# Layer 0's mixers: two PSUM banks for a head's output, two instead of three for transposed probabilities

## The chip, the cores and the metric

The kernel runs on one core of a Trainium2 chip. The metric is the device time of one execution in microseconds (us); smaller is better. Engines are named as in the profile: PE is TensorE's matmul, PEld its weight load, DVE is VectorE, ACT ScalarE, POOL GpSimd, SP SyncE, which issues the loads and stores.

## The reference

An encoder trunk of two layers on x of 2048 tokens by 1024, all in float32. Only layer 0 is touched by the change:

```python
def even_layer(x, norm_g, w_in, w_out, a_qn, a_kn, a_sinks, b_qn, b_kn, b_rel, cos, sin):
    h = rms_norm(x, norm_g)
    aq, ak, av, ag, bq, bk, bv, bg = jnp.split(h @ w_in, cuts, axis=-1)
    ...  # QK-norm of both mixers, rotary for A
    ya = sliding_window_sink_attention(aq, ak, av, a_sinks) * jax.nn.silu(ag)  # own + 2 chunks of 64
    yb = chunked_relbias_attention(bq, bk, bv, b_rel) * jax.nn.silu(bg)        # own + 8 chunks of 64
    return x + jnp.concatenate([ya, yb], axis=-1) @ w_out
```

Mixer A has 8 query heads over 2 key/value heads, mixer B 8 heads; a head has 64 dimensions. Layer 1 is a differential attention over all earlier chunks, with its own projections.

## The kernel before

Each float32 operand of a large matmul is split into a high half (rounded) and a low half (the rest), and a product is made of two or three matmuls of these. Layer 0 first projects (lines up to L470), then `_mix0` runs both mixers and the output projection; then comes layer 1.

`_mix0` goes over 4 blocks of 512 tokens, and in each over 16 heads, alternating two of A and two of B. A head has a score part and a value part. The score part (`scores_a`, `scores_b`) makes scores in PSUM (tiles mSA, mSB, L567 and L568), takes the row maximum on DVE (L617, L698), the exponential on ACT (L622, L704) and scales on POOL (L628, L706), into mPA and mPB. The value part (`values_a`, `values_b`) goes over the key tiles of 128: PE transposes up to four 128x128 pieces of probabilities into one PSUM bank (tile mtrA or mtrB, L656 and L721); `split_pt` has ACT write the high half (mptH, L573) and DVE the low half (mptL, L574), each into one of three buffers in SBUF; then two value matmuls, with the high half (L663, L725) and with the low half (L665, L726), add into the head's output (mOA or mOB), 128x512, one PSUM bank. After a head's last key tile `join` adds the two 64-row halves of the output: ACT copies one (mlow, L581), DVE adds the other (myt, L582). POOL multiplies by the gate (L587), and `split_y` makes myH and myL (L593, L594).

The output projection of the block before (tile mom, 24 matmuls a tile, L214 to L216, evicted by DVE at L486) and some late gate tiles (mlg) run beside this, as `side`. `pace` writes the program: it takes score parts, lets the value parts trail by LAG0 units, and adds side units by SHARE0. The order on each engine is then set by a scheduler, which places an instruction by its own reckoning of when its operands and its buffers will be there; a PSUM tile gets a bank of its pool when the bank's last reader is past. So the number of banks in a pool also moves the order. Each engine runs its list in order.

PSUM has eight banks, and `BANKS0` deals them out in `_mix0`: NS to scores, NTR to transposed probabilities, NO to a head's output, NM to the side work. In the last block, every other output tile of the projection (j odd) takes its bank from the pool of head outputs.

Of the kernel before, what the change touches and what calls it, by code (L numbers as in the profile page):

```python
# [85 lines left out]
class Trunk:  # L86
    LATE = 8
    AHEAD = 2
    BANKS0, LAG0, SHARE0 = (3, 3, 1, 1), 9, 0.85
    FIN = 18  # L90
    COMB = 5
    BANKS1, LAG1 = (4, 2, 1, 1), (20, 36, 36, 36)
# [1106 lines left out]
```

## Time and profile before

| what | value |
|---|---|
| median of 3 runs (lowest to highest) | 2917.48 us (2905.52 to 2921.39) |
| the profiled execution, and its span | 2905.78 us, 2903.8 us |
| mean granted clock of PE | 0.973 |
| layer 0's projection | up to about 604 us |
| layer 0's mixers and output projection | 604 to about 1209 us |
| layer 1 | from about 1210 us |
| PE's 128-column transposes of probabilities | 560 (B) + 248 (A) |

All durations below are from the one profiled execution. A line of the profile names line, engine, operation and tiles as out<-in; a wait names who waited and for whom. A matmul's duration in the trace contains a modelled tail that overlaps the next matmul, so the time that a matmul costs PE (its slot) is read from start to start.

### The profile page before, as it was taken

The numbers are of one execution on the slowest core, as the hardware profiler recorded it, in microseconds if no ns is written. First come the engines' busy times: TensorE is split into PE (matmuls) and PEld (weight loads), VectorE is DVE, ScalarE is ACT, GpSimd is POOL, SyncE is SP. The second block draws the span as 40 slices with busy tenths as digits, with TensorE's granted clock in tenths as the row PEclk, the third lists the DMA queues.
The fourth block names the chain that finished last, engine by engine and source line by source line (L and its number), as shares of the span: only waits on it lengthen the run. The fifth ranks groups of instructions, "written<-read, shape, count | busy, mean of one in ns | idle before, by whom it ended". The sixth has DMA issues, their size and how long they took to land.

```text
span 2903.8 us, 45243 instructions
## 1 busy us (share of the span) xinstructions
PE 2718.9 (94%) x13704; PEld 2244.2 (77%) x13704; DVE 1950.6 (67%) x4685; ACT 1597.0 (55%) x4135; POOL 1612.4 (56%) x1968
## 2 busy tenths in 40 slices
PE   6999999998899999899999999999999999899889
PEld 5788888887787888777788887777777777677667
DVE  7762385257787885598729861666667888879842
ACT  4443543367666665343344321667667777678752
POOL 4541251334544354267745640777777777789851
PEclk9999999999999999999999999999999999999999
DMA  4673344648877763567894454786777677668873
GB/s 149 226 245 138 117 137 131 198 131 236 217 196 178 193 175 109 189 218 235 264 298 167 131 175 146 235 225 188 203 215 215 188 228 213 173 170 250 209 227 116
DMA packets 408866, 555.83 MB, mean 191 GB/s; under 512 B 47152, under 2 KB 187184, under 8 KB 408624
## 3 DMA queue, kind: packets, MB, share of 16 engines
q1 hardware_dynamic: 408624, 552.96, 64.7%
q8 instruction: 109, 1.79, 0.3%
q14 instruction: 133, 1.09, 0.1%
HBM read 388.18 MB, written 164.63 MB: 190 GB/s over the span
## 4 chain that ended last, share of the span: by engine, by line
PE 71%; DVE 11%; DMA 10%; ACT 4%; issue 2%; POOL 1%; SPq 1%; DVEq 0%; ACTq 0%; POOLq 0%
PE p1mm L216 5%; PE p1mm L214 5%; PE p1mm L215 5%; PE p0mm L214 3%; PE p0mm L215 3%; PE p0mm L216 3%; PE cS L883 3%; PE cS L884 3%; PE ctr L931 3%; PE cG L214 2%; PE cG L216 2%; PE cG L215 2%; PE cO L940 2%; PE com L214 2%; PE com L215 2%
## 5 line engine op out<-in xcount | busy, mean ns | idle before, releaser
L890 ACT ACTIVATE cP<-cS,cnm 128x512 f32<-128x512 f32 (+3 forms) x640 | 398.0, 628 | 147.3 <-DVE cnm L887 99.9
L887 DVE TENSOR_REDUCE cnm<-cS 128x1 f32<-128x512 f32 (+3 forms) x640 | 375.3, 600 | 98.1 <-PE cS L884 93.1
L304 POOL TENSOR_TENSOR p0wL<-p0ws,p0wH 128x512 fp32r<-128x512 f32 (+1 forms) x128 | 155.5, 1247 | 271.3 <-ACT p0wH L303 261.9
L883 PE MATMUL cS<-ck,cqd 128*128 128x512 f32 (+3 forms) x640 | 264.5, 417 | 42.4 <-ACT cP L890 19.0
L214 PE MATMUL p1mm<-p1wH,p1hH 128*128 128x512 f32 x768 | 303.1, 396 | 0.7 <-ACT p1wH L303 0.7
L215 PE MATMUL p1mm<-p1wL,p1hH 128*128 128x512 f32 x768 | 303.3, 395 | 0.4 <-POOL p1wL L304 0.4
L216 PE MATMUL p1mm<-p1wH,p1hL 128*128 128x512 f32 x768 | 303.6, 396 | 0.0
L918 POOL TENSOR_TENSOR cP<-cP,cP 128x512 f32<-128x512 f32 (+3 forms) x256 | 285.1, 1135 | 0.3
L304 POOL TENSOR_TENSOR p1wL<-p1ws,p1wH 128x512 fp32r<-128x512 f32 x128 | 167.6, 1329 | 140.5 <-ACT p1wH L303 116.1
L884 PE MATMUL cS<-ck,cql 128*128 128x512 f32 (+3 forms) x640 | 238.0, 376 | 7.0 <-DMA cql<-qL 6.9
L214 PE MATMUL p0mm<-p0wH,p0hH 128*128 128x512 f32 (+1 forms) x640 | 237.7, 374 | 3.5 <-ACT p0vt L454 2.6
L215 PE MATMUL p0mm<-p0wL,p0hH 128*128 128x512 f32 (+1 forms) x640 | 238.1, 373 | 0.0
L216 PE MATMUL p0mm<-p0wH,p0hL 128*128 128x512 f32 (+1 forms) x640 | 237.8, 373 | 0.1
L935 DVE TENSOR_TENSOR cptL<-ctr,cptH 128x512 fp32r<-128x512 f32 (+1 forms) x320 | 190.7, 599 | 51.3 <-ACT cptH L934 50.5
L934 ACT ACTIVATE cptH<-ctr 128x512 fp32r<-128x512 f32 (+1 forms) x320 | 169.9, 538 | 67.5 <-PE ctr L931 66.5
L912 POOL TENSOR_SCALAR cP<-cP,ccs 128x512 f32<-128x512 f32 (+3 forms) x288 | 191.9, 684 | 0.0
L883 PEld LDWEIGHTS cS<-ck,cqd 128*128 128x128 f32 x640 | 124.7, 195 | 83.1 <-ACT cP L890 42.3
L931 PE MATMUL ctr<-ident,cP 128*128 128x128 f32 x1088 | 175.9, 277 | 5.5 <-DVE cP L915 3.7
L917 POOL TENSOR_SCALAR cP<-cP,ccs 128x512 f32<-128x512 f32 (+3 forms) x256 | 170.6, 679 | 0.0
L214 PEld LDWEIGHTS p1mm<-p1wH,p1hH 128*128 128x128 f32 x768 | 145.8, 190 | 29.8 <-ACT p1wH L303 1.0
L215 PEld LDWEIGHTS p1mm<-p1wL,p1hH 128*128 128x128 f32 x768 | 145.6, 190 | 29.9 <-POOL p1wL L304 0.8
L216 PEld LDWEIGHTS p1mm<-p1wH,p1hL 128*128 128x128 f32 x768 | 145.8, 190 | 29.1 <-issue 0.2
(325 smaller groups left out, 7767.5 us busy)
## 6 DMA issues: line engine op xcount, KB each, us to landing
p1ws<-in_od_w_in_dram SPq DMA_DIRECT2D x56, 512.0 KB, 4.9
p0ws<-in_ev_w_in_dram SPq DMA_DIRECT2D x48, 512.0 KB, 4.3
ck<-kH SPq DMA_DIRECT2D x160, 128.0 KB, 4.4
ck<-kL SPq DMA_DIRECT2D x160, 128.0 KB, 4.4
cvH<-vH SPq DMA_DIRECT2D x80, 256.0 KB, 4.8
cvL<-vL SPq DMA_DIRECT2D x80, 256.0 KB, 4.3
cqd<-qH SPq DMA_DIRECT2D x128, 128.0 KB, 4.7
cql<-qL SPq DMA_DIRECT2D x128, 128.0 KB, 4.5
```

Of the source, the lines that this page charges most:

```text
L214: mm(ps, aH, bH, start=first, stop=False)
L215: mm(ps, aH, bL, start=False, stop=False)
L216: mm(ps, aL, bH, start=False, stop=last)
L304: nc.gpsimd.tensor_tensor(l[:, :width], ws[:, k, :width], f32(h[:, :width]), ALU.subtract)
L883: mm(ps, qd[:, m, js], kt[:, :wd], start=True, stop=False)
L884: self.anchor = mm(ps, ql[:, m, js], kt[:, :wd], start=False, stop=True).ins
L887: nc.vector.tensor_reduce(nm[:, m, z:z + 1], ps, AX.X, ALU.max, negate=True)
L890: nc.scalar.activation(chunks[z][:, :wd], ps, AF.Exp, bias=nm[:, m, z:z + 1], accum_out=acc)
L912: nc.gpsimd.tensor_scalar(p1, p1, c1, 1.0, ALU.mult, ALU.mult)
L918: nc.gpsimd.tensor_tensor(p1, p1, p2, ALU.add)
L931: nc.tensor.transpose(tp[:, (j - j0) * P:(j - j0 + 1) * P], us[j][kt // 4][:, kk:kk + P], self.ident)
L935: nc.vector.tensor_tensor(L[:, :wd], tp[:, :wd], f32(H[:, :wd]), ALU.subtract)
```

## The change

One tuple changes: the transposed probabilities get two banks instead of three, the heads' outputs two instead of one. Scores (3) and side work (1) keep theirs.

```diff
 class Trunk:
     LATE = 8
     AHEAD = 2
-    BANKS0, LAG0, SHARE0 = (3, 3, 1, 1), 9, 0.85
+    BANKS0, LAG0, SHARE0 = (3, 2, 2, 1), 9, 0.85
     FIN = 18
```

No instruction is added or removed; the scheduler gives another order from the first mixer heads to layer 1's start, and for a stretch near the end of layer 1.

First place: PE, where a head of A (mOA_8694) ends and a head of B (mOB_8793) begins, in the second block. Before (L721 transposes, L725 and L726 are value matmuls, L567 and L568 scores of another head):

```order
L665 MATMUL mOA_8694<-mptL_8765,mvA_7851 128x128
L721 MATMUL mtrB_8836<-ident_89,mPB_8542 128x128
L721 MATMUL mtrB_8836<-ident_89,mPB_8581 128x128
L721 MATMUL mtrB_8836<-ident_89,mPB_8633 128x128
L567 MATMUL mSB_9138<-mks_9085,mqd_9079 128x384
L568 MATMUL mSB_9138<-mks_9085,mql_9082 128x384
L721 MATMUL mtrB_8852<-ident_89,mPB_8542 128x128
L721 MATMUL mtrB_8852<-ident_89,mPB_8581 128x128
L721 MATMUL mtrB_8877<-ident_89,mPB_8542 128x128
L725 MATMUL mOB_8793<-mptH_8799,mvB_8536 128x512
L726 MATMUL mOB_8793<-mptL_8800,mvB_8536 128x512
```

Then L725 and L726 of the second tile follow, and those of mtrB_8836 (mptH_8840, mptL_8841). The same head in the new order:

```order
L725 MATMUL mOB_8793<-mptH_8799,mvB_8536 128x512
L726 MATMUL mOB_8793<-mptL_8800,mvB_8536 128x512
L721 MATMUL mtrB_8836<-ident_89,mPB_8542 128x128
L721 MATMUL mtrB_8836<-ident_89,mPB_8581 128x128
L721 MATMUL mtrB_8836<-ident_89,mPB_8633 128x128
L725 MATMUL mOB_8793<-mptH_8813,mvB_8536 128x512
L726 MATMUL mOB_8793<-mptL_8814,mvB_8536 128x512
L721 MATMUL mtrB_8852<-ident_89,mPB_8542 128x128
L721 MATMUL mtrB_8852<-ident_89,mPB_8581 128x128
L725 MATMUL mOB_8793<-mptH_8840,mvB_8536 128x384
L726 MATMUL mOB_8793<-mptL_8841,mvB_8536 128x384
```

The transposes of a tile have moved behind the first value matmuls of their head, and the value matmuls that use them stand two rows of other work later instead of a whole group.

Second place: ACT at the same head. Before:

```order
L573 ACTIVATE mptH_8799<-mtrB_8794 128x512
L573 ACTIVATE mptH_8813<-mtrB_8808 128x512
L581 ACTIVATE mlow_8787<-mOA_8694 64x512
L573 ACTIVATE mptH_8840<-mtrB_8836 128x384
L573 ACTIVATE mptH_8855<-mtrB_8852 128x256
```

And now:

```order
L573 ACTIVATE mptH_8799<-mtrB_8794 128x512
L581 ACTIVATE mlow_8787<-mOA_8694 64x512
L573 ACTIVATE mptH_8813<-mtrB_8808 128x512
L573 ACTIVATE mptH_8840<-mtrB_8836 128x384
L573 ACTIVATE mptH_8855<-mtrB_8852 128x256
```

The join of the head before stands one split earlier; it is still among the next head's splits.

Third place: DVE at the stage's end, where layer 1's rotary tables (p1tqC and so on) and layer 0's last evictions (L486) share the engine. Before:

```order
L187 TENSOR_TENSOR p1tkS_14942<-p1sin_14929,od_k_norm_103 128x16x32
L188 TENSOR_TENSOR p1tkS_14942<-p1sin_14929,od_k_norm_103 128x16x32
L486 TENSOR_TENSOR mxr_14651<-mom_14653,mxr_14651 128x512
L486 TENSOR_TENSOR mxr_14680<-mom_14682,mxr_14680 128x512
L191 TENSOR_SCALAR p1tqS_14933<-p1tqS_14933 128x16x32
```

And now:

```order
L187 TENSOR_TENSOR p1tkS_14942<-p1sin_14929,od_k_norm_103 128x16x32
L188 TENSOR_TENSOR p1tkS_14942<-p1sin_14929,od_k_norm_103 128x16x32
L191 TENSOR_SCALAR p1tqS_14933<-p1tqS_14933 128x16x32
L205 TENSOR_SCALAR p1xms_14957<-p1xss_14953 128x1
L193 TENSOR_SCALAR p1tqS_14933<-p1tqS_14933 128x16x32
L206 SCALAR_TENSOR_TENSOR p1xu_14958<-p1xy0_14956 128x1
L486 TENSOR_TENSOR mxr_14651<-mom_14653,mxr_14651 128x512
```

Four short rows of layer 1 have moved ahead of the first of these evictions.

## The prediction

> **What bounds the kernel now.** First the page: the span, the engines' busy time, and the shares of the chain that ended last.
>
> ```profile
> span 2903.8 us, 45243 instructions
> PE 2718.9 (94%) x13704; PEld 2244.2 (77%) x13704; DVE 1950.6 (67%) x4685; ACT 1597.0 (55%) x4135; POOL 1612.4 (56%) x1968
> PE 71%; DVE 11%; DMA 10%; ACT 4%; issue 2%; POOL 1%; SPq 1%; DVEq 0%; ACTq 0%; POOLq 0%
> ```
>
> PE sets the time. The change touches one stage only, so next comes the table of stretches: layer 0's mixers (604 to 1209 us), three slices of them, and a stretch near the kernel's end. Columns: stretch, length, busy time of PE, PEld, DVE, ACT and POOL, granted clock, DMA share, GB/s.
>
> ```profile
> 604.00:1209.00 605.00, 553.54 (x3280) 478.86 (x3279) 440.63 (x1502) 377.71 (x1003) 260.96 (x390) 0.96 0.70 182
> 750.00:780.00 30.00, 24.55 (x138) 21.54 (x139) 20.00 (x75) 14.62 (x35) 11.16 (x18) 0.89 0.74 205
> 780.00:810.00 30.00, 28.58 (x184) 25.07 (x183) 24.36 (x85) 20.95 (x57) 10.69 (x17) 1.00 0.73 192
> 1170.00:1209.00 39.00, 37.86 (x163) 31.17 (x164) 13.01 (x29) 4.92 (x12) 0.00 (x0) 0.91 0.35 125
> 2750.00:2800.00 50.00, 40.68 (x185) 31.24 (x186) 28.48 (x87) 32.38 (x89) 41.10 (x63) 0.90 0.73 202
> ```
>
> In the mixers PE is busy 553.5 of 605 us; DVE (441) and ACT (378) are behind it by far. So only what makes PE wait counts there. Who makes it wait, in the list of waits between 604 and 1160 us (total us, times, longest):
>
> ```profile
> PE mSA L567 <- ACT mPA L622: 7.6, 7, 2.1
> PE mOB L725 <- DVE myt L582: 6.6, 18, 0.9
> PE mom L216 <- POOL myL L594: 5.6, 1, 5.6
> PE mtrB L721 <- DVE mptL L574: 5.0, 13, 0.8
> PE mOB L726 <- DVE mptL L574: 0.9, 1, 0.9
> PEld mOB L725 <- DVE myt L582: 11.5, 21, 1.3
> PEld mtrB L721 <- DVE mptL L574: 9.0, 17, 1.1
> ACT mptH L573 <- PE mOB L725: 27.3, 25, 7.3
> ```
>
> The second row is the bank of a head's output: the first value matmul of a head (L725) waits until DVE has read the head before out of the single bank. The fourth is the bank of transposed probabilities: a transpose (L721) waits until DVE has made the low half (mptL) from the tile that stood there. The last shows that with three such banks ACT runs ahead of PE: 25 times its high half (mptH) waits for a buffer that an older value matmul still reads. The value matmuls therefore find their operands ready: the fifth row, 0.9 us, is the only one of them that waits for a half.
>
> **What the change removes.** Here is one of the 18 waits, in the timeline (start, us, engine, what, idle before):
>
> ```profile
> 789.30 0.22 PE L665 MATMUL mOA<-mptL,mvA 128*128 128x128 f32 x1
> 789.36 0.50 PE L721 MATMUL mtrB<-ident,mPB 128*128 128x128 f32 x3
> 789.57 0.59 ACT L581 ACTIVATE mlow<-mOA 64x512 f32<-64x512 f32 x1
> 789.61 0.42 PE L567 MATMUL mSB<-mks,mqd 128*128 128x384 f32 x1
> 789.87 0.33 PE L568 MATMUL mSB<-mks,mql 128*128 128x384 f32 x1
> 790.04 0.73 PE L721 MATMUL mtrB<-ident,mPB 128*128 128x128 f32 x3
> 790.19 0.49 ACT L573 ACTIVATE mptH<-mtrB 128x384 fp32r<-128x384 f32 x1
> 790.42 0.69 DVE L582 TENSOR_TENSOR myt<-mOA,mlow 64x512 f32<-64x512 f32 x1
> 791.14 0.56 DVE L574 TENSOR_TENSOR mptL<-mtrB,mptH 128x384 fp32r<-128x384 f32 x1
> 791.16 0.50 PE L725 MATMUL mOB<-mptH,mvB 128*128 128x512 f32 x1 [0.40 <-DVE myt L582]
> 791.73 0.39 PE L725 MATMUL mOB<-mptH,mvB 128*128 128x512 f32 x1
> 791.96 0.39 PE L726 MATMUL mOB<-mptL,mvB 128*128 128x512 f32 x1
> ```
>
> Mixer A's head ends at 789.30, is joined by ACT (0.59) and DVE (0.69), and only at 791.16 may the next head start. The same rows give PE's slots, start to start: 512 columns 0.23 us (791.73 to 791.96), 384 columns 0.17 (789.87 to 790.04), so 256 and 128 columns 0.12 and 0.06 in proportion. A transpose takes 0.11: three last 0.50, of which the last one's own length is 0.27:
>
> ```profile
> L721 PE MATMUL mtrB<-ident,mPB x560: 270/273/478, 619.1 to 1155.7; 128*128 128x128 f32 x187
> ```
>
> Slots between the two heads: six transposes and two of 384 columns, 6 x 0.11 + 2 x 0.17 = 1.0 us. The join needs 0.17 (a last matmul's length beyond its slot, 0.22 to 0.27 less 0.06 to 0.11) + 0.59 + 0.69 + 0.1 for hand-overs = 1.56. Shortfall 0.56, of which the trace counts 0.40 as idle, since 0.17 is still the last matmul's modelled length. So I add 0.17 to each counted wait: 6.6 + 18 x 0.17 = 9.6 us for the output bank (the weight loads' row says 11.5). With two banks the next head writes the other one; by the order a bank then comes round after 2.9 us of slots or more, so this goes to zero, all but the wait at the stage's end for the very last head.
>
> **What it adds.** The counts stay: 312 transposed tiles, 808 transposes, 752 value matmuls, no operation more or less. But a tile's bank must be empty two tiles later instead of three, and the order follows: transposes are issued later, next to the value matmuls that use them (the two orders of PE above show this on the very place of the rows just quoted). What was cover is gone. The chain of a tile, from these rows (idle in the last column):
>
> ```profile
> L573 ACT ACTIVATE mptH<-mtrB 128x512 fp32r<-128x512 f32 x56 | 32.7, 599 | 17.7 <-PE mtrB L721 11.4 <-PE mOA L663 6.1
> L573 ACT ACTIVATE mptH<-mtrB 128x384 fp32r<-128x384 f32 x56 | 27.4, 489 | 13.3 <-PE mtrB L721 5.2 <-DVE mptL L574 5.0 <-DVE mbnm L700 1.9
> L573 ACT ACTIVATE mptH<-mtrB 128x256 fp32r<-128x256 f32 x56 | 21.4, 381 | 26.3 <-PE mOB L725 24.2 <-PE mtrB L721 1.7
> L573 ACT ACTIVATE mptH<-mtrB 128x128 fp32r<-128x128 f32 x56 | 15.2, 271 | 8.2 <-PE mtrB L721 4.2 <-PE mOB L725 2.9
> L574 DVE TENSOR_TENSOR mptL<-mtrB,mptH 128x512 fp32r<-128x512 f32 x56 | 38.0, 689 | 14.3 <-ACT mptH L573 9.0 <-PE mOA L663 4.2
> L574 DVE TENSOR_TENSOR mptL<-mtrB,mptH 128x384 fp32r<-128x384 f32 x56 | 30.8, 551 | 3.4 <-ACT mptH L573 2.8
> L574 DVE TENSOR_TENSOR mptL<-mtrB,mptH 128x256 fp32r<-128x256 f32 x56 | 23.5, 419 | 9.2 <-ACT mptH L573 9.1
> L574 DVE TENSOR_TENSOR mptL<-mtrB,mptH 128x128 fp32r<-128x128 f32 x56 | 15.8, 283 | 5.2 <-ACT mptH L573 4.4 <-PE mOB L726 0.8
> ```
>
> High half: 0.17 + ACT + 0.07 = 0.83, 0.72, 0.62, 0.51 us for 512, 384, 256, 128 columns after the last transpose's slot. Low half: 0.17 + ACT + DVE + 0.1 = 1.55, 1.30, 1.07, 0.82. At the place shown, after the change the third tile (384 columns) has between its transposes and its high half's matmul two value matmuls of 512 and two transposes: 0.46 + 0.22 = 0.68 us against 0.72; the low half comes 0.17 later, at 0.85 against 1.30. So PE waits 0.04, then 0.41, where before it had 2 x 0.17 + 3 x 0.11 + 4 x 0.23 = 1.6 us of slots in between and waited for neither half.
>
> I did this count along all of the stage's some 3,280 PE rows in both orders: each row gets its slot, a row that comes too early for its tile's half, or for a bank, waits the shortfall, and all behind it moves. Before: 3 tile-bank waits of 2.9 us, 15 output-bank waits of 8.0, and 0.5 for halves: 11.4 us. After: 49 waits for a high half (7.5 us), 68 for a low half (20.0), and the one at the end (1.6): 29.1 us. Net +17.7, with each chain as short as its rows.
>
> They aren't that short. In the rows above the tile transposed at 789.36 gets its high half only at 790.19, since ACT first does the join's mlow, and its low half at 791.14, behind DVE's myt: from the end of its slots (789.69) to 791.70 are 2.0 us, against 1.30. That costs nothing before; in the new order the join still stands among the splits. Before's measured waits say how much longer a chain is on average: 9.6 (outputs) + 5.0 + 13 x 0.17 = 7.2 (tile banks) + 1.6 at the end = 18.4 us, which the count gives if every chain is 1.22 times its rows. With the same factor the new order counts 46.4 us. Net **+28 us**. Both ends: the chains as short as 0.82 of the rows (next part) give +11; the weight loads' 11.5 + 9.0 + 1.6 = 22.1 ask for a factor of 1.32, and the new order then has 56: +34; doubling for ACT and DVE being busier around the splits than a mean factor tells, at 1.5: 74.7 - 30.8 = +44.
>
> **Other moves.** At the stage's end layer 0's last output tiles now go over three banks instead of two. PE stops there in either order, because DVE has layer 1's rotary tables (L185 to L193) ahead of the evictions (L486):
>
> ```profile
> 1171.03 0.80 PE L214 MATMUL mom<-mw,myH 128*128 128x512 f32 x1 [5.87 <-DVE mxr L486]
> 1171.62 0.63 PE L215 MATMUL mom<-mw,myH 128*128 128x512 f32 x1
> ```
>
> After the last head PE has 30 rows before it needs an evicted bank, where it had 27: 3 x 0.23 = 0.7 us less idle; DVE has four short rows more in front of the first eviction. I cost the two at nothing together; the ends are the whole 5.87 gained and as much lost. SP's and POOL's issues are the same in number and change places; PE's waits for loads and for POOL aren't moved by a rule that I can see, so nothing, with the 5.6 us of the single wait for myL as the end on both sides. The last 100 us of layer 1 are ordered a little differently too; the idle 9.3 us of the 50 at 2750 bound what can be won or lost there.
>
> **The sum.** The profiled execution took 2905.8 us (2903.8 of it the span); with 28 us more, 2934. It lies at the lower edge of the runs, 11.7 under their median of 2917.5. Against the median the forecast is 2945.5, and I give that.
>
> **The rivals.**
> First, no change: the cover is longer than slots tell. The stage took 605 us for some 495 us of slots, so rows stand 605/495 = 1.22 times further apart than counted, which is the same as chains of 0.82 of their rows. The new order then waits 17.2 us, the old one 6.3 by the count but 18.4 as measured: between -1 and +11, about 2922. For it speaks that ACT is idle 37% of the stage; against it that stretch by idle time sits in a few gaps (5.87 and 5.6 in two places), not between a tile's transposes and its matmuls.
> Second, faster: the output bank's waits vanish and the splits hold up nobody, because ACT, no longer stopped by PE's late buffers (its 27.3 us), starts every split at once. The place is the three or four tiles at each head's change. It decides where chains fall below about 0.75 of their rows: the count gives 9.7 us at 0.7. At best 9.6 + 7.2 us go, 2917.5 - 17 = 2900. Against it: the join still shares ACT and DVE with the first tiles of the next head.
> Third, much slower: many short stops take PE's clock down. After the 5.87 us of idle just shown a matmul has 0.63 where the rows at 791 have 0.39, and its slice has a clock of 0.91; the slice at 750, just behind the 5.6 us wait, has 0.89. In the slice at 780, with the 0.40 wait in it, the clock is 1.00, so short stops did no harm there. If ten such slices of the stage fell to 0.89, they would lose 30 x 0.11 = 3.3 us apiece: 2945 + 33 = 2978.
> The Trainium skill (TensorE: Matmul & The Clock Gate, "A second HAM failure mode: psum-queue depth-cycling") states that cycling through PSUM banks can make PE pause between groups often enough for its clock to swing between half and full. By that rule the third rival is the likely one; the slice at 780 doesn't bear it out for pauses of this length.
>
> **How the numbers follow.** Chances: the forecast 0.54, no change 0.23, faster 0.11, much slower 0.12. A measurement of this kernel tells 0.5% (15 us) from no change; so slower 0.66, same 0.23, faster 0.11. The forecast's own range is +17.7 to +44, 2935 to 2962. The range takes in no change and the upper bound, and leaves out the better part of the faster rival (about 0.07, below 2910) and the worst of the much slower one (0.10, above 2972).
>
> **What would show it.** After: no PE row waits for myt but the one at the stage's end; new rows of PE (L725, L726, L663, L665) waiting for mptH and mptL, over 100 in number and 25 to 55 us in all with weight loads; ACT's 27.3 us for PE's buffers mostly gone; the stage some 630 us long, with PE's busy time about the same. I am wrong if these waits stay under 15 us, if the stage's clock falls clearly under 0.96, or if a difference of over 10 us comes from layer 1.

## The result, and the profile after

The changed kernel takes 2948.12 us (median of 6 runs, 2934.14 to 2951.8) against 2908.24 us for the kernel before in the same rounds (2901.79 to 2921.39). The ratio is 1.0112, with a 95% interval of [1.0083, 1.0142]: slower by 1.1%. Profiled a second time, with rounds of its own, it gave 1.0103 [1.0075, 1.0131] (below). The profiled execution took 2951.8 us.

The page's three lines after the change:

```profile
span 2950.0 us, 45103 instructions
PE 2746.1 (93%) x13704; PEld 2251.3 (76%) x13704; DVE 1941.1 (66%) x4685; ACT 1601.6 (54%) x4135; POOL 1614.8 (55%) x1968
PE 64%; DVE 12%; DMA 9%; ACT 5%; issue 2%; POOL 2%; SPq 1%; ACTq 0%; DVEq 0%; POOLq 0%
```

The span grew by 46.2 us. In the chain that ended last, PE's share fell from 71 to 64%, and ACT's, DVE's and POOL's rose by a point each. The stretches of the mixers, and the slice at 780 us (columns as before: stretch, length, busy PE, PEld, DVE, ACT, POOL, clock, DMA share, GB/s):

```profile
604.00:1238.00 634.00, 574.50 (x3284) 483.49 (x3283) 436.99 (x1507) 385.95 (x1008) 262.37 (x390) 0.97 0.68 176
780.00:810.00 30.00, 27.46 (x167) 22.92 (x167) 23.01 (x77) 19.31 (x52) 11.71 (x18) 1.00 0.80 197
```

From the first mixer matmul to layer 1's first one the stage takes 633.6 us, where it took 605.7: +27.9. (All stage lengths below are between these two rows of one profiled execution each.) The clock did not fall: 0.97 against 0.96. The slice at 780 got 167 PE rows done where it got 184.

Who makes PE and its weight loads wait there now (total us, times, longest):

```profile
PE mOA L665 <- DVE mptL L574: 11.4, 21, 1.4
PE mOB L726 <- DVE mptL L574: 5.6, 22, 0.6
PE mOB L725 <- ACT mptH L573: 5.2, 11, 2.1
PE mOA L663 <- ACT mptH L573: 3.0, 5, 0.7
PE mom L214 <- DVE mxr L486: 5.3, 1, 5.3
PE mom L214 <- DVE myt L582: 1.4, 1, 1.4
PEld mOB L726 <- DVE mptL L574: 19.6, 46, 1.2
PEld mOA L665 <- DVE mptL L574: 15.9, 22, 1.7
PEld mOB L725 <- ACT mptH L573: 12.7, 27, 2.4
PEld mOA L663 <- ACT mptH L573: 6.7, 16, 1.0
ACT mptH L573 <- PE mtrB L721: 73.5, 92, 5.0
```

The waits for the output bank are gone but one of 1.4 us, which is the stage's end. In their place stand waits of the value matmuls for their halves: 25.2 us in 59 waits on PE (before, one of 0.9), 54.9 us in 111 on the weight loads (before, 1.7). And ACT has changed sides: the 27.3 us of its idle time that ended when PE gave a buffer back are gone, and the row that ends when PE has made a tile grew from 22.4 to 73.5 us. ACT no longer runs ahead of PE.

A warning on reading this: PE's idle time in the stage hardly moved, 605.0 - 553.5 = 51.5 us before and 634.0 - 574.5 = 59.5 after, although the stage lost 28 us with the same work. The rest went into "busy", which rose by 21 us. The same head as in the prediction's timeline shows how:

```profile
793.61 0.39 PE L725 MATMUL mOB<-mptH,mvB 128*128 128x512 f32 x1
793.62 0.69 DVE L582 TENSOR_TENSOR myt<-mOA,mlow 64x512 f32<-64x512 f32 x1
793.84 0.40 PE L726 MATMUL mOB<-mptL,mvB 128*128 128x512 f32 x1
794.07 0.49 PE L721 MATMUL mtrB<-ident,mPB 128*128 128x128 f32 x3
794.32 0.48 PE L725 MATMUL mOB<-mptH,mvB 128*128 128x512 f32 x1
794.35 1.33 DVE L574 TENSOR_TENSOR mptL<-mtrB,mptH 128x512 fp32r<-128x512 f32 x2
794.60 0.49 ACT L573 ACTIVATE mptH<-mtrB 128x384 fp32r<-128x384 f32 x1 [0.49 <-PE mtrB L721]
795.09 0.51 PE L726 MATMUL mOB<-mptL,mvB 128*128 128x512 f32 x1 [0.29 <-DVE mptL L574]
795.44 0.38 PE L721 MATMUL mtrB<-ident,mPB 128*128 128x128 f32 x2
```

From the high half's matmul at 794.32 to the low half's at 795.09 are 0.77 us, where its slot is 0.23: 0.54 us lost. The trace shows 0.29 of it as idle; the rest is the 0.48 that the waiting pair's first matmul is drawn long. So short waits are read from start to start, or from the weight loads. The 54.9 us alone are not the loss, since other waits became shorter: all waits of the weight loads in the stage add up to 75.0 us before and 99.0 after, and this growth of 24.0 stands against the stage's 27.9. What is late here is DVE: it made myt, the join of the head before, from 793.62 to 794.31, and only then the two low halves.

A small part of the stage's loss is something else. Layer 1's first matmul (p1mm) waits for the high half of its weights (p1wH), which ACT makes; before, then after:

```profile
1210.64 0.96 PE L214 MATMUL p1mm<-p1wH,p1hH 128*128 128x512 f32 x3 [0.74 <-ACT p1wH L303]
1238.31 1.65 PE L214 MATMUL p1mm<-p1wH,p1hH 128*128 128x512 f32 x3 [3.34 <-ACT p1wH L303]
```

ACT now has two rows of layer 1's norm (L317) ahead of that half. From the last matmul of the output projection to this one the step is 6.4 us, where it was 4.2: 2.2 of the 27.9 us. So the new order doesn't end at layer 1's start: up to about 85 us into layer 1 the engines' rows are in another order too.

### The profile page after: what moved, and what is told of

The parts are those of the page before. It is cut to its first block, busy times and chain, and to the rows that moved or that the text cites. A ratio compares the mean times of both kernels' runs of the same rounds, so it can differ in the third digit from the quotient of the medians.

```text
span 2950.0 us, 45103 instructions
## 1 busy us (share of the span) xinstructions
PE 2746.1 (93%) x13704; PEld 2251.3 (76%) x13704; DVE 1941.1 (66%) x4685; ACT 1601.6 (54%) x4135; POOL 1614.8 (55%) x1968
## 4 chain that ended last, share of the span: by engine, by line
PE 64%; DVE 12%; DMA 9%; ACT 5%; issue 2%; POOL 2%; SPq 1%; ACTq 0%; DVEq 0%; POOLq 0%
PE p1mm L216 4%; PE p1mm L214 4%; PE p1mm L215 4%; PE cS L883 3%; PE cS L884 3%; PE ctr L931 3%; PE p0mm L214 3%; PE p0mm L215 3%; PE p0mm L216 3%; PE mom L214 2%; PE cG L214 2%; PE cO L940 2%; PE mom L216 2%; PE cG L216 2%; PE mom L215 2%
```

## Experiments

Each kernel changes the kernel before, except where it says otherwise. Ratios are against the kernel before in the same rounds, with their 95% intervals. The numbers in BANKS0 are the banks for scores, transposed probabilities, head outputs and side work.

**The changed kernel again**, for what an execution adds by itself.

> The changed kernel once more. In its first profile the mixers' stage (604 us to the first matmul of layer 1's projection) was 28 us longer than before, and layer 1 took 18 us more as well, though its instructions stand in the same order up to its last 100 us. If the stage's loss comes from the order of PE's rows, it is +26 to +30 again. If layer 1's 18 us belong to the kernel, they come again within 4 us; if they belong to that one execution, layer 1 differs by 8 us or more from the first profile.

Measured: 1.0103 [1.0075, 1.0131], 2939.32 against 2910.19 us. The stage took 631.7 us (+26.0). Layer 1's projection took 590.3 us (before 584.6, first profile of the change 589.1) and its attention 1111.5 (1108.6 and 1122.6). So of the 18.5 us that layer 1 had over before in the first profile 8.7 are left; the stage's loss stands.

**The transposes' bank alone taken away**, the output keeping its one bank:

```diff
-    BANKS0, LAG0, SHARE0 = (3, 3, 1, 1), 9, 0.85
+    BANKS0, LAG0, SHARE0 = (3, 2, 1, 1), 9, 0.85
```

> One part alone: two banks for transposed probabilities, still one for a head's output (an eighth bank lies idle). My theory (a tile bank less takes the cover between transposes and value matmuls): waits counted along the new order are 44 us with chains as short as their rows, of which 25 for the output bank, 10 for the halves and 8 for tile banks, and 66 us at 1.22 times; before they were 13 and 21. So the stage is 31 to 45 us longer than before, worse than with both parts. Rival (the second output bank is what hurts, since it lets heads' value parts run into each other): within 5 us of before.

Measured: 1.0154 [1.0117, 1.019], 2953.93 us, and a stage of 646.9 us, +41. Its stretch, then its waits:

```profile
603.00:1250.00 647.00, 574.81 (x3281) 482.42 (x3281) 439.19 (x1507) 382.41 (x1010) 261.21 (x390) 0.97 0.66 172
```

```profile
PE mOA L663 <- DVE myt L582: 23.3, 23, 2.2
PE mOB L725 <- DVE myt L582: 8.1, 12, 1.5
PE mOB L725 <- ACT mptH L573: 5.5, 26, 0.6
```

One bank less for transposes costs all of the loss and more. Most of it shows here as waits for the single output bank: 31.4 us, where they were 6.6. The value matmuls wait only 5.9 us for halves. Given two banks for transposes, the second output bank is worth 646.9 - 633.6 = 13.3 us. So the change can be read as a loss of 41 and a gain of 13, though the waits stand in other rows in the two kernels.

**The output's second bank taken from the scores** instead:

```diff
-    BANKS0, LAG0, SHARE0 = (3, 3, 1, 1), 9, 0.85
+    BANKS0, LAG0, SHARE0 = (2, 3, 2, 1), 9, 0.85
```

> The other part alone, its bank taken from the scores: banks (2, 3, 2, 1). My theory: waits for the output bank are gone, waits for halves are 3 to 8 us, and what it costs are score banks (8 to 15 us): 11 to 23 us in all against 13 to 21 before, so the stage is within 5 us of before. Rival (the second output bank hurts): value matmuls wait for mptH and mptL some 25 us as in the changed kernel, the stage 20 us or more longer.

Measured: 0.9946 [0.9924, 0.9968], 2893.0 us: faster, with a stage of 585.0 us (-20.7). That is better than expected. (The value matmuls' waits for halves, expected at 3 to 8 us, came to 14.5 on PE.) The stretch and the waits of this kernel:

```profile
604.00:1190.00 586.00, 548.10 (x3284) 474.94 (x3283) 437.39 (x1507) 377.04 (x1010) 261.43 (x391) 0.97 0.71 191
```

```profile
PE mOB L726 <- DVE mptL L574: 9.7, 14, 4.3
PE mSB L567 <- ACT mPA L622: 2.5, 5, 0.9
PE mSA L567 <- ACT mPA L622: 1.8, 3, 1.2
```

The expectation charged 8 to 15 us to the lost score bank. But the waits for score banks became fewer: 4.3 us in these two rows, where before the first of them was

```profile
PE mSB L567 <- ACT mPA L622: 6.1, 4, 2.6
```

and the second 7.6, in all 13.7. The two longest single waits of before are not in the new list either: 5.6 us for myL, and 5.87 at the stage's end. Why two score banks wait less than three was not tried; the other order is the likely place. What this run does show is that a second output bank doesn't hurt where the transposes keep three: PE has no wait for an output bank left. How much of the 20.7 us is that bank, and how much the other order, it doesn't show.

**The low half left out**, with the old banks (first) and the new ones (second). Transposed probabilities then have no low half, and both value matmuls read the high one:

```diff
-            L = sb.tile([P, 512], F32R, tag="ptL", name=n + "ptL", bufs=3)
...
-            nc.vector.tensor_tensor(L[:, :wd], ps[:, :wd], f32(H[:, :wd]), ALU.subtract)
-            return H, L
+            return H, H
```

> Banks as before (3, 3, 1, 1), and the low half of the transposed probabilities is left out: DVE's L574 is gone, and the second value matmul takes the high half again, so PE's rows keep their number and sizes. A tile's chain is ACT's copy alone, 0.83 us instead of 1.55 for 512 columns. It is the partner of the next run; counted waits 5 to 8 us. All theories expect the stage to be some 5 to 15 us shorter than before.

> The same with the changed kernel's banks (3, 2, 2, 1). My theory (the loss is the tile's chain ACT then DVE seen by PE): with the chain halved the counted waits are 7 to 13 us, 3 to 5 more than in the partner, so the stage is within 6 us of the partner's instead of 26 to 28 longer. Rival (the loss comes from the order itself or from the second output bank, whatever the chain): 20 us or more longer than the partner.

Measured, once each: 2873.1 us with the old banks, 2882.94 with the new; stages of 575.2 and 580.6 us.

```profile
604.00:1180.00 576.00, 539.49 (x3285) 475.12 (x3284) 322.47 (x1193) 378.35 (x1007) 260.52 (x391) 0.97 0.72 192
```

```profile
607.00:1188.00 581.00, 548.82 (x3283) 474.52 (x3282) 325.88 (x1194) 378.03 (x1007) 261.27 (x390) 0.98 0.72 190
```

```profile
PE mOB L723 <- ACT mptH L572: 5.0, 12, 1.5
PE mOA L661 <- ACT mptH L572: 3.2, 6, 0.9
```

With the chain cut to its first half the change costs 5.4 us, not 27.9. So most of the loss needs the whole chain of ACT and then DVE: neither the banks' cycling as such nor the transposes' being next to the value matmuls makes it alone. The 5.4 us are a net figure. The weight loads still wait 24.7 us in 58 waits for the high half (1.5 in the run with the old banks, 54.9 in the changed kernel), and against this the run with the old banks has waits that the other lacks, such as 7.1 us of PE for myL. DVE also has 118 us less to do in the stage here, which these two runs don't separate from the shorter chain.

**The join's reader of the bank on DVE freed from ACT.** ACT's copy of the lower rows and DVE's read of the upper ones were to run side by side, with the sum on POOL:

```diff
-            nc.vector.tensor_tensor(yt[hi, :], O[hi, :], tmp[hi, :], ALU.add)
+            nc.vector.tensor_scalar(yt[hi, :], O[hi, :], 1.0, None, ALU.mult)
+            nc.gpsimd.tensor_tensor(yt[hi, :], yt[hi, :], tmp[hi, :], ALU.add)
```

> Banks as before (3, 3, 1, 1), but the join frees the output bank sooner: ACT copies one half and DVE the other side by side, and POOL adds them from SBUF (64 instructions of POOL more, some 80 us of its time, of which it has 340 free in the stage). A bank comes free after 0.17 + 0.69 + 0.1 = 0.96 us instead of 1.56. If the 18 waits of PE for myt were worth their 9.6 us, they go nearly to zero (1 to 3 us left) and the stage gets 8 to 10 us shorter, 0.3%. Rival (such waits are only moved to the next wait, or POOL's longer chain to the gate holds up the output projection): the stage is within 2 us of before.

Measured: 1.0011 [0.9996, 1.0027], 2914.82 us, stage 604.9. Nothing was won, because the edit did not shorten the join. Its timeline at the same head (from L582 on, this kernel's lines are one higher than before's), and its waits:

```profile
833.81 0.60 ACT L581 ACTIVATE mlow<-mOB 64x512 f32<-64x512 f32 x1
834.44 0.68 DVE L582 TENSOR_SCALAR myt<-mOB 64x512 f32<-64x512 f32 x1
835.18 0.50 PE L726 MATMUL mOB<-mptH,mvB 128*128 128x512 f32 x1
```

```profile
PE mOB L726 <- DVE myt L582: 6.6, 18, 0.5
```

DVE reads other rows of the bank than ACT and needs nothing of ACT's, and still it starts 0.03 us after ACT ends (833.81 + 0.60). The 18 waits and their 6.6 us are what they were. The trace says who imposes the turn: DVE's read waits for a semaphore, a signal between engines, that ACT raises when it ends. None of the 64 reads begins before ACT's copy has ended, and in 11 of the waits DVE stood idle until then, 9.0 us in all. So the program orders the two reads; whether they could run side by side was not tried. The run says nothing on what a shorter join would bring.

**The join with a single reader of the bank.** ACT copies the whole output out of PSUM once; the rest is done from SBUF:

```diff
-            nc.scalar.activation(tmp[hi, :], O[lo, :], AF.Copy)
-            nc.vector.tensor_tensor(yt[hi, :], O[hi, :], tmp[hi, :], ALU.add)
+            nc.scalar.activation(tmp, O, AF.Copy)
+            nc.scalar.activation(yt[hi, :], tmp[lo, :], AF.Copy)
+            nc.gpsimd.tensor_tensor(yt[hi, :], yt[hi, :], tmp[hi, :], ALU.add)
```

> Banks as before (3, 3, 1, 1). The join in which DVE and ACT were to read the output bank side by side still had DVE start only when ACT had ended, and PE's 18 waits for myt stayed at 6.6 us, so it told nothing of their worth. Here ACT alone reads the bank, once, 128x512 (0.6 us), copies a half from SBUF again, and POOL adds. The bank is free after 0.17 + 0.60 + 0.07 = 0.84 us; DVE loses 64 instructions of 0.69 us, ACT gains 64 of 0.6. If the waits were worth their 9.6 us, PE has none of them longer than 0.2 us and the stage is 8 to 14 us shorter (counted waits 3 to 8 instead of 13 to 21). Rival (the time turns up in other waits, ACT's longer queue above all): within 3 us of before.

Measured: 0.9946 [0.9925, 0.9968], 2888.24 against 2906.79 us; stage 586.8 (-18.9).

```profile
604.00:1191.00 587.00, 543.56 (x3292) 476.54 (x3290) 411.53 (x1450) 410.47 (x1078) 341.42 (x454) 0.97 0.71 190
```

```profile
PE mOB L726 <- ACT mlow L581: 2.8, 5, 1.0
```

The output bank's waits fell from 6.6 to 2.8 us without a second bank, at 33 us more of ACT and 80 more of POOL, both off the path. The stage gained twice the 9.6 us that the prediction gave these waits. But not all of it is the bank. Of the two longest single waits of before, 5.6 us for myL and 5.87 at the stage's end, 0.4 and 2.2 us are left in their rows, while others came, one of 5.4 for a low half among them. DVE is also freed of the joins among the low halves. These were not taken apart.

**The same join with the changed banks**, (3, 2, 2, 1):

> The changed kernel's banks (3, 2, 2, 1) with the join in which ACT reads the output bank once and POOL adds. The join's DVE instruction no longer stands among the splits. My theory (the third tile bank was the cover): counted waits are 31 to 51 us against 3 to 8 in its partner with (3, 3, 1, 1), so its stage is 25 to 35 us longer than the partner's 586.8 us: 612 to 622. Rival (the changed kernel lost because the join of one head delays the next head's splits on DVE and ACT): with that taken away it is within 10 us of the partner.

Measured: 1.0056 [1.0037, 1.0074], 2920.68 against 2903.88 us; stage 615.7, that is +28.9 over the same join with the old banks.

```profile
PE mOA L666 <- DVE mptL L574: 15.7, 23, 2.0
PE mOA L664 <- ACT mptH L573: 7.4, 8, 1.5
PE mOB L727 <- DVE mptL L574: 4.7, 17, 1.4
PEld mOB L727 <- DVE mptL L574: 26.0, 69, 1.9
```

The join is no longer in DVE's way, and the waits for halves are more in sum: 28.7 us on PE where they were 25.2, 60.7 on the weight loads where they were 54.9. So the chain is late by its own length in an order that leaves it no cover; DVE's join among the splits is a part of single waits, as at 793.62 above, but not of the sum. ACT has a copy more for each head here, so this clears DVE's part of the join and not ACT's.

**A fourth transposes' bank**, from the scores:

```diff
-    BANKS0, LAG0, SHARE0 = (3, 3, 1, 1), 9, 0.85
+    BANKS0, LAG0, SHARE0 = (2, 4, 1, 1), 9, 0.85
```

> Banks (2, 4, 1, 1). Scores with two banks, transposed probabilities with four, one for outputs. The version (2, 3, 2, 1) had a stage 21 us shorter than before. If its gain came from the second output bank, this one lacks it: waits for myt are there again and the stage is within 5 us of before. Rival (its gain came from scores having two banks, which makes the scheduler space the heads otherwise, whatever the freed bank does): the stage is 15 us or more shorter here too.

Measured: 0.9982 [0.9963, 1.0], 2899.95 us; stage 594.9 (-10.8).

```profile
PEld mOB L725 <- DVE myt L582: 2.4, 4, 0.9
PE mtrB L721 <- POOL mPB L706: 11.6, 7, 3.8
```

This lies between what the two theories gave and does not tell them apart. The weight loads' waits for the output bank fell from 11.5 to 2.4 us in this row though it is still a single bank, and transposes issued earlier now wait for POOL's probabilities.

**The two gains together**: the join with a single reader and banks (2, 3, 2, 1).

> Both improvements together: banks (2, 3, 2, 1) and the join of ACT and POOL. With the short join the second output bank has little left to give (counted output waits 0 either way), and the score banks cost what they cost: stage between 575 and 590 us, thus about the better of the two alone (585.0 and 586.8). If the two gains were of different kinds and added up, it would be 566 us.

Measured: 0.9915 [0.9887, 0.9943], 2878.82 against 2903.88 us; stage 576.1. It is the fastest of the runs that keep the low half.

```profile
605.00:1182.00 577.00, 542.97 (x3284) 473.26 (x3283) 400.52 (x1443) 407.32 (x1074) 341.86 (x455) 0.98 0.71 194
```

| banks | join of before | join with a single reader |
|---|---|---|
| (3, 3, 1, 1) | 605.7 | 586.8 |
| (3, 2, 2, 1) | 633.6, 631.7 | 615.7 |
| (3, 2, 1, 1) | 646.9 | not run |
| (2, 3, 2, 1) | 585.0 | 576.1 |
| (2, 4, 1, 1) | 594.9 | not run |

Stage lengths in us. The step from the first row to the second is +28 and +29: there the join makes no difference. The step from the first to the fourth is -20.7 and -10.7: those two gains overlap.

## Why the prediction was right, and where not

- **The stage's term, +28 us: right.** It measured +27.9 and +26.0. The count with chains of their own rows gave +17.7 and was too low; the factor of 1.22 drawn from before's waits hit. There is luck in how well it hit. Measured as before's 18.4 us were, by PE's idle time and 0.17 for each wait, the new waits are 25.2 + 59 x 0.17 + 1.6 = 36.8, which makes +18. By the weight loads they are 54.9 + 1.5 = 56.4 against 22.1, which makes +34; that is what the count gave at a factor of 1.32. The stage lies between, and moves that the prediction put at nothing are in it: the scores' waits for ACT's mPA fell from 13.7 to 6.8 us on PE, the one for myL from 5.6 to 2.6, and the one for p1wH rose from 0.7 to 3.3.
- **The total: near, in part by luck.** 2945.5 was forecast and 2948.12 measured. But the forecast stood on before's first median, 2917.48; with the later rounds it is 2908.24. Of the 40 us between the medians (33 by the ratio) 28 were forecast; the rest lies in layer 1.
- **The mechanism: shown.** The new waits stand where they were forecast, at the value matmuls. Cutting the chain takes most of the loss away (+5.4); taking the join off DVE does not (+28.9). Taking the bank away alone costs more (+41), though there most of the waits are for the output bank.
- **Output bank, -9.6 us: the right kind, its size not shown.** The waits vanished as said. Beside two transposes' banks a second output bank was worth 13.3 us. With three, no run gave it by itself: (2, 3, 2, 1) also moves a score bank, and the 18.9 us of the single-reader join also have the two long waits in them that went.
- **"PE's busy time about the same": wrong.** It rose by 21 us, with the same matmuls at about the same clock (0.97 and 0.96), because part of each short wait is drawn as a long matmul, as at 794.32 above. The step that failed is the reading of the modelled tail: it was allowed for in the size of a wait (0.17 each; 111 x 0.17 would be 19 us), not in the busy time.
- **The place.** The wait was forecast on the third tile, 0.04 and then 0.41 us; it stands on the second tile's low half, 0.54 start to start, because DVE was still joining. The third tile's two matmuls follow at 795.58 and 795.83 without a wait. The count took DVE and ACT as free and put their being busy into one factor; that is good for a sum over a stage, not for a single place.
- **The stage's end, nothing: right for the evictions, not for the last step.** The stop was 5.87 us before and is 5.3 after. The 2.2 us in front of layer 1's first matmul were not forecast.
- **Layer 1, nothing: not borne out in full.** It took 18.5 us more in the first profile and 8.7 in the second. The rows of layer 1 from its start (columns as above), before and then after, split where its projection ends:

```profile
1210.60:1795.20 584.60, 574.13 (x2663) 473.04 (x2664) 402.43 (x700) 218.93 (x493) 332.93 (x256) 0.99 0.63 207
1795.20:2903.80 1108.60, 1019.47 (x4930) 812.28 (x4928) 786.76 (x1793) 738.87 (x2049) 806.61 (x1120) 0.96 0.72 204
```

```profile
1238.30:1827.40 589.10, 574.42 (x2663) 472.74 (x2664) 402.45 (x697) 217.16 (x490) 332.86 (x256) 0.99 0.62 203
1827.40:2950.00 1122.60, 1025.29 (x4930) 814.76 (x4929) 782.99 (x1793) 739.18 (x2049) 805.67 (x1120) 0.96 0.71 201
```

  The same work took 14.0 us longer in the attention and 4.5 in the projection, at the same clocks. Over all ten experiments the attention took 1101.7 to 1125.2 us, and 1125.2 came with the join of DVE's copy, whose stage was as long as before. So most of this is the execution. Of the 40 us between the medians (33 by the ratio) the stage explains 28, and 5 to 12 are left to layer 1. About 5 us more in the projection came in both profiles of the change (4.5 and 5.7). They are idle time of PE (14.7 us in the projection, 10.4 before) and go with the order at layer 1's start, not with the banks. In before and three other kernels p1mm first waits 0.7 to 1.0 us for p1wH, and the projection takes 582.5 to 584.6 us; two of these have the banks (3, 2, 2, 1). In all others that wait is 2.5 to 3.9 us and the projection takes 585.2 to 590.4, also with old banks (589.8 in the run with DVE's copy). No run changed that order by itself. The prediction looked for new orders in layer 1 only near its end. By its own words ("a difference of over 10 us comes from layer 1") the prediction would have been wrong in the first profile and not in the second.
- **The rivals.** No change (cover longer than slots tell) and faster (splits hold up nobody) fall with the 54.9 us of waits. Much slower falls by the clock: 111 waits of the weight loads, none over 2.4 us, and the stage at 0.97. The Trainium skill (TensorE: Matmul & The Clock Gate, "A second HAM failure mode: psum-queue depth-cycling") describes a clock that swings because PE pauses between groups while cycling through banks; that was not seen for pauses of this length.

## What to carry to other kernels

A bank in a ring between two engines is time: the third transposes' bank covered a chain of ACT and then DVE of about 1.55 us at 512 columns, and the output bank a join of the same length, but a tile has that chain five times as often as a head has the join (312 tiles, 64 heads). Before trading banks, count for each pool how often its chain runs and what stands between its write and its use, and look for the pool that can give one up (here the scores') or for an edit that shortens the hold on the scarce bank (one reader, the rest from SBUF). Read short waits of a pipelined PE from start to start or from all waits of its weight loads together, since PE's idle time showed 8 of 28 us and the weight loads' sum 24. And before a stage's gain is put down to one bank, look which long single waits came or went with the new order.

## What had not been expected of the hardware

These runs show no new behaviour of the chip that a reader should carry away. What looked like one, ACT and DVE taking turns on one PSUM bank (833.81 + 0.60, then 834.44), is a wait of DVE for ACT's semaphore, and so the program's own order.
